# Layer-0 attention stored class by class, two out-projection seams in a new order, and one weight place fewer

## The chip, the cores and the metric

The kernel runs on one core of a Trainium2 chip. The core has a matrix engine (TensorE, in the trace PE, with its weight loads as PEld), a vector engine (VectorE, DVE), an activation engine (ScalarE, ACT), a general engine (GpSimd, POOL), and SyncE (SP), which here only issues DMAs. The engines run their own instruction streams and meet at semaphores. On-chip memory is SBUF (128 partitions), and matmuls write PSUM. The metric is the device time of one execution in microseconds (us); lower is better.

## The reference

Two pre-norm residual layers over 1024 tokens of width 1024, then a final norm. Layer 0 mixes tokens with 12 heads of dilated window attention and a gated MLP; layer 1 with two kinds of dense attention. Each layer ends in a mixture of 16 experts in which experts choose tokens. The part that the change touches most is the dilated attention:

```python
A_PATTERNS = ((128, 1), (512, 4), (2048, 16))
...
def dilated_band_attention(q, k, v, window, dilation):
    """Centred dilated window: query t attends t + j*dilation, |j| <= window/(2*dilation).
...
def dilated_mixture(q, k, v):
    results = [dilated_band_attention(q, k, v, w, d) for (w, d) in A_PATTERNS]
    outs = jnp.stack([o for (o, _) in results], axis=0)
    lses = jnp.stack([l for (_, l) in results], axis=0)
    wts = jax.nn.softmax(lses, axis=0)
    return jnp.einsum('pbsh,pbshc->bshc', wts.astype(q.dtype), outs)
...
def mixer_even(h, pos, w_in, gmlp_norm, w_s, b_s, w_out):
    ...
    return jnp.concatenate([a_out, g_out], axis=-1) @ w_out
...
    for i in range(DEPTH):
        h = rmsnorm(x, norm_mix[i])
        ...
        x = x + mix
        x = x + ec_moe(rmsnorm(x, norm_ffn[i]), moe_w_router[i], moe_w_gate[i], moe_w_up[i], moe_w_down[i])
    return rmsnorm(x, final_norm)
```

## The kernel before

**Products.** float32 operands are split into a high and a low part (`split`: ACT copies the high part, DVE or POOL subtracts for the low one), and a product is three matmuls: high x high, low x high, high x low (L259 to L261). Weights come from HBM in pieces of 128x1024 through a ring of SBUF places; `Stream.load` issues a piece's DMA on SP as soon as a place is free, and `Stream.conv` makes its two parts (L225 hi on ACT, L232 lo on DVE, or on POOL with `pool=True`).

**Attention of layer 0** (`a_attention`). The patterns with dilation 4 and 16 fall together on the positions of one residue class modulo 4, so a head has two kinds of 128-query blocks: eight natural ones (neighbouring positions) and eight class ones (positions r, r+4, r+8 ...; two blocks for each of 4 residues). One unit is two blocks, so a head has 8 units: s < 4 are class units, s >= 4 natural ones. For each unit PE computes scores (`emit_S`, L1190, tile ass: per block two matmuls of 128x256, against the two halves kT[:, 0] and kT[:, 1] of the split keys), DVE masks and takes the maximum (L1192, tile sm), ACT exponentiates (L1199, pe), PE transposes (L1206, apP), ACT copies to SBUF (L1208, pT), and PE multiplies by the values (`emit_PV`, L1220, apO), which come in natural order (vn) and in class order (vc). The hand-written loop over t runs these steps skewed by a unit or two, so that engines work on different units.

The queries and keys of a pair of heads are loaded into qs and ks in natural order (`a_keys`). `prep` splits them for each head (ksp, qsp), transposes them on PE (tile apt) and copies the result to kT and qT (L1139 on DVE, L1141 on ACT); two DMAs (`a_swap`) exchange the halves of kT. In kT and qT positions are in natural order, so a natural unit reads them contiguously, and a class unit reads every fourth element, which is a step of 16 bytes:

```python
out.append((qT.rearrange("p (l r) -> p r l", r=4)[:, r, j * 128:(j + 1) * 128],
            [kT[:, f, 64:64 + S].rearrange("p (l r) -> p r l", r=4)[:, r] for f in range(2)],
```

When a pair is done, its class results go through DRAM into natural order (`bounce`: o2d, then tile o2, shown as o), and `merge` (L1244 to L1272) weighs the natural and the class result by their softmax sums into the tile attn. The merge of an earlier pair is spread over steps of the next; that of the last pair stands behind the loop in two slices of token chunks.

**Seam to the out-projection of layer 0.** The out-projection (`out_moe`, tile pp) multiplies the transposed attn (aTh, aTl, from `mix.part`: PE transposes, L148 and L149 split) by the output weights. Their first pieces are converted in the last steps of attention; four more low parts are made by POOL (`pool=layer == 0`). The first token chunk's products begin with the columns that earlier pairs have filled, and need the last pair's merge from the fifth 128 columns on.

**Seam to the out-projection of layer 1.** Dense attention (`odd_attention`) has 128 blocks: scores css (L1873), maximum (L1879), exponential pe (L1885), transposes cpt, the split PT (L148 and L149), and PV into po (L1915, L1916) in groups of four blocks; L1921 and L1923 add the two halves (ol, o), and the reciprocal row sums rinv go through DRAM (rd, rb). The transposed results lie in DRAM: oda for 14 heads (7 chunks of 128 rows), odb for the last two. `OddMix.load` brings a token chunk back as aT (L1983 for oda, L1984 for odb), into the out-projection's own pool, and `OddMix.part` splits it. The odd output weights' parts lie in three slots of the tile cT.

**Ring places.** The ring has `n_ring = 7` places; further places are added for each layer (8 in layer 0, 15 in layer 1, from the pool ringa), and buffers that have become free join.

## Time and profile before

| | |
|---|---|
| median of 3 runs | 2000.86 us (2000.85 to 2000.86) |
| profiled execution | 1999.71 us, of it 1997.9 us span |
| mean granted TensorE clock | 0.968 of full |
| PE busy | 1864.8 us (93%) |
| DVE, ACT, POOL busy | 1473.5, 1244.9, 352.4 us |

The profile is one execution. The span runs from the first to the last instruction. Busy time is the time in which an engine executed something; the idle time in front of an instruction is put down to the event that ended it. An instruction's line can be that of a helper, so that L232 is the low part of any weight piece and L148 any split.

### The profile page before, as it was taken

The numbers are of one execution on the slowest core, as the hardware profiler recorded it, in microseconds if no ns is written. First come the engines' busy times: TensorE is split into PE (matmuls) and PEld (weight loads), VectorE is DVE, ScalarE is ACT, GpSimd is POOL, SyncE is SP. The second block draws the span as 40 slices with busy tenths as digits, with TensorE's granted clock in tenths as the row PEclk, the third lists the DMA queues.
The fourth block names the chain that finished last, engine by engine and source line by source line (L and its number), as shares of the span: only waits on it lengthen the run. The fifth ranks groups of instructions, "written<-read, shape, count | busy, mean of one in ns | idle before, by whom it ended". The sixth has DMA issues, their size and how long they took to land. (4 is left out here: it accounts for less than half of the span.)

```text
span 1997.9 us, 29943 instructions
## 1 busy us (share of the span) xinstructions
PE 1864.8 (93%) x10346; PEld 1568.7 (79%) x10346; DVE 1473.5 (74%) x3160; ACT 1244.9 (62%) x2022; POOL 352.4 (18%) x337
## 2 busy tenths in 40 slices
PE   8999999998995999998999799999997995999995
PEld 6888899997883788886888688888886873888884
DVE  6431246777557999997776688889996558999997
ACT  5322257776232888886634688889885334888884
POOL 0010010002002321211002233322212003212111
PEclk9999999999996999999899899999998997999997
DMA  7232354543473999995426554332213875999986
GB/s 236 69 106 75 116 153 130 140 108 109 158 261 126 377 389 384 385 395 156 134 70 202 114 75 90 60 50 42 53 22 93 288 256 201 391 387 385 387 332 229
DMA packets 214599, 386.32 MB, mean 193 GB/s; under 512 B 71984, under 2 KB 122928, under 8 KB 214448
## 3 DMA queue, kind: packets, MB, share of 16 engines
q1 hardware_dynamic: 190224, 303.95, 46.0%
q0 software_dynamic: 21488, 74.18, 12.2%
q10 hardware_dynamic: 2736, 6.29, 0.9%
q8 instruction: 81, 1.33, 0.3%
q14 instruction: 70, 0.57, 0.2%
HBM read 310.17 MB, written 66.85 MB: 189 GB/s over the span
## 5 line engine op out<-in xcount | busy, mean ns | idle before, releaser
L232 DVE TENSOR_TENSOR lo<-raw,hi 128x1024 fp32r<-128x1024 f32 x260 | 310.1, 1227 | 24.2 <-ACT hi L225 23.0
L225 ACT ACTIVATE hi<-raw 128x1024 fp32r<-128x1024 f32 x269 | 275.2, 1055 | 14.5 <-PE py L643 10.2
L259 PE MATMUL pp<-hi,hT 128*128 128x512 f32 (+2 forms) x576 | 213.4, 371 | 2.3 <-ACT hi L235 2.3
L260 PE MATMUL pp<-lo,hT 128*128 128x512 f32 (+2 forms) x576 | 211.8, 368 | 0.1
L261 PE MATMUL pp<-hi,hT 128*128 128x512 f32 (+2 forms) x576 | 211.4, 367 | 0.0
L1879 DVE TENSOR_REDUCE nm<-css 128x1 f32<-128x1024 f32 x128 | 156.0, 1218 | 41.5 <-PE css L1873 40.8
L149 DVE TENSOR_TENSOR PT<-cpt,PT 128x512 fp32r<-128x512 f32 x256 | 163.1, 678 | 6.1 <-ACT PT L148 3.8
L148 ACT ACTIVATE PT<-cpt 128x512 fp32r<-128x512 f32 x256 | 139.5, 597 | 42.1 <-PE cpt L1897 40.3
L1873 PE MATMUL css<-kT,qT 128*128 128x512 f32 x512 | 151.7, 398 | 10.7 <-ACT pe L1885 9.5
L1885 ACT ACTIVATE pe<-css,nm 128x1024 f32<-128x1024 f32 x128 | 143.6, 1122 | 11.0 <-DVE rinv L1905 7.1
L1897 PE MATMUL cpt<-csident,pe 128*128 128x128 f32 x1024 | 135.5, 275 | 1.0 <-DVE PT L149 0.9
L1897 PEld LDWEIGHTS cpt<-csident,pe 128*128 128x128 f32 x1024 | 117.1, 141 | 16.3 <-DVE PT L149 3.7
L1915 PE MATMUL po<-PT,vv 128*128 128x512 f32 x256 | 113.4, 443 | 13.2 <-DVE o L1923 13.2
L259 PEld LDWEIGHTS pp<-hi,hT 128*128 128x128 f32 x576 | 109.7, 190 | 19.8 <-ACT hi L235 2.7
L260 PEld LDWEIGHTS pp<-lo,hT 128*128 128x128 f32 x576 | 109.6, 190 | 17.8 <-DVE lo L236 0.8
L261 PEld LDWEIGHTS pp<-hi,hT 128*128 128x128 f32 x576 | 109.4, 190 | 17.5 <-DVE hT L149 0.2
L1873 PEld LDWEIGHTS css<-kT,qT 128*128 128x128 f32 x512 | 96.0, 189 | 34.6 <-ACT pe L1885 10.8
L1192 DVE CUSTOM_DVE_ANT_0 sm<-ass,csnat 128x256 f32<-128x256 f32 x176 | 67.3, 420 | 52.0 <-PE ass L1190 45.9
L578 POOL DMA_INDIRECT xs<-hd,idx x32 | 70.2, 2195 | 197.5 <-DVE gt L576 197.5
L1916 PE MATMUL po<-PT,vv 128*128 128x512 f32 x256 | 102.3, 400 | 0.0
L1190 PE MATMUL ass<-kT,qT 128*128 128x256 f32 x384 | 96.4, 381 | 1.0 <-DMA kT<-kT 1.0
L259 PE MATMUL pp<-hi,aTh 128*128 128x512 f32 x208 | 87.3, 420 | 0.4 <-DVE o L1226 0.4
(435 smaller groups left out, 4656.0 us busy)
## 6 DMA issues: line engine op xcount, KB each, us to landing
raw<-in_moe_w_up_dram SPq DMA_DIRECT2D x112, 512.0 KB
raw<-in_moe_w_down_dram SPq DMA_DIRECT2D x110, 512.0 KB
raw<-in_moe_w_gate_dram SPq DMA_DIRECT2D x106, 512.0 KB
attn<-in_moe_w_gate_dram SPq DMA_DIRECT2D x22, 512.0 KB
attn<-in_moe_w_down_dram SPq DMA_DIRECT2D x18, 512.0 KB
raw<-in_even_w_in_dram SPq DMA_DIRECT2D x16, 512.0 KB
hd<-h POOLq DMA_DIRECT2D x16, 512.0 KB, 6.0
attn<-in_moe_w_up_dram SPq DMA_DIRECT2D x16, 512.0 KB
```

Of the source, the lines that this page charges most:

```text
L148: self.nc.scalar.activation(hi, src, AF.Copy)
L149: (eng or self.nc.vector).tensor_tensor(lo, src, hi.bitcast(F32), op=ALU.subtract)
L225: nc.scalar.activation(hv, tv, AF.Copy)
L232: (nc.gpsimd if pool else nc.vector).tensor_tensor(lv, tv, hv.bitcast(F32), op=ALU.subtract)
L259: nc.tensor.matmul(out, ah, bh, start=first, stop=False)
L260: nc.tensor.matmul(out, ah, bl, start=False, stop=False)
L261: nc.tensor.matmul(out, al, bh, start=False, stop=last)
L1873: nc.tensor.matmul(ss[:, n], a[:, sl], m[:, n * 512:(n + 1) * 512], start=(j == 0), stop=(j == len(passes) - 1))
L1879: nc.vector.tensor_reduce(nm, B[b]["ss"], axis=AX.X, op=ALU.max, negate=True)
L1885: nc.scalar.activation(pe, B[b]["ss"], AF.Exp, bias=B[b]["nm"], accum_out=l)
L1897: nc.tensor.transpose(pt[:, kk], B[b]["pe"][:, kc * 128:(kc + 1) * 128], k.ident)
L1915: nc.tensor.matmul(po[g], vv[:, kc], PT[g][:, 0, kc], start=(kc == 0), stop=False)
```

## The change

First, layer 0's attention is stored class by class. Queries and keys are loaded in class order (four DMAs for ks, then four for qs, instead of one each), so kT and qT hold the four residue classes one behind the other, kT with 16 zero elements on both sides of each class. A class unit reads contiguous columns. A natural unit reads its keys as runs of 32 elements, its mask's columns and its values' rows are permuted to that order (vn comes by 12 DMAs instead of 3), and its queries come from a second copy qN, which is written back into natural order, every fourth element (for head 0 on DVE, for the other 11 heads on ACT, two copies each).

Second, at the seam to layer 0's out-projection POOL makes one low part and DVE the others, and the last merge is cut after 2 chunks instead of 4. Third, at the seam to layer 1's out-projection aT gets a pool of its own (mixa), and the load from oda is issued inside attention, at `late[-4]`. Fourth, the ring has 6 places; layer 0 gets 9 instead of 8 further ones, layer 1 15 as before.

```diff
+    wk = 128 * (w // 128) + 4 * (w % 32) + w % 128 // 32
...
-        add(name, np.where(ok, 0.0, NEG))
+        add(name, np.where(ok, 0.0, NEG)[:, wk])
...
-            stream.conv(base + (4 if layer else 8), pool=layer == 0, load=False)
+            if layer == 0:
+                stream.conv(base + 5, pool=True, load=False)
+            stream.conv(base + (4 if layer else 7), load=False)
...
+PAD = 16
...
-    nc.sync.dma_start(qs, src[:, c:c + 128].rearrange("(c p) d -> p c d", p=128))
-    nc.sync.dma_start(ks, src[:, w + c:w + c + 128].rearrange("(c p) d -> p c d", p=128))
+    for t, c0 in ((ks, w + c), (qs, c)):
+        v = src[:, c0:c0 + 128].rearrange("(f p r) d -> p r f d", f=2, r=4)
+        for r in range(4):
+            nc.sync.dma_start(t[:, 2 * r:2 * r + 2], v[:, r])
...
-    nc.gpsimd.memset(vn[0:64, 0], 0.0)
-    nc.gpsimd.memset(vn[64:128, 8], 0.0)
+    nc.gpsimd.memset(vn[:, 0], 0.0)
+    nc.gpsimd.memset(vn[:, 8], 0.0)
...
-    nc.sync.dma_start(vn[64:128, 0], vv[0:64])
-    nc.sync.dma_start(vn[:, 1:8], vv[64:960].rearrange("(c p) d -> p c d", p=128))
-    nc.sync.dma_start(vn[0:64, 8], vv[960:1024])
+    for r in range(4):
+        p = 32 * r
+        nc.sync.dma_start(vn[p + 16:p + 32, 0], vv[0:64].rearrange("(l r) d -> r l d", r=4)[r])
+        nc.sync.dma_start(vn[p:p + 32, 1:8], vv[64:960].rearrange("(c l r) d -> r l c d", l=32, r=4)[r])
+        nc.sync.dma_start(vn[p:p + 16, 8], vv[960:1024].rearrange("(l r) d -> r l d", r=4)[r])
...
-        nc.sync.dma_start(*(kT[p:p + 64, f, 64:64 + S].bitcast(F32) for p, f in ((64 - a, 1), (a, 0))))
+        nc.sync.dma_start(*(kT[p:p + 64, f, :, PAD:PAD + 256].bitcast(F32) for p, f in ((64 - a, 1), (a, 0))))
+def a_pads(nc, kT):
+    nc.vector.memset(kT[:, :, :, 0:PAD].bitcast(F32), 0.0)
+    nc.vector.memset(kT[:, :, :, PAD + 256:].bitcast(F32), 0.0)
+def two(v):
+    return v.rearrange("p (r l) -> p r l", r=2)
...
-    kT, qT = take("kT", 2, 128 + S, dtype=F32R), take("qT", S, dtype=F32R)
+    kT, qT, qN = take("kT", 2, 4, 2 * PAD + 256, dtype=F32R), take("qT", S, dtype=F32R), take("qN", S, dtype=F32R)
...
-    pair, head = dict(qs=qs, ks=ks, cls=cls), dict(kT=kT, qT=qT)
+    pair, head = dict(qs=qs, ks=ks, cls=cls), dict(kT=kT, qT=qT, qN=qN)
...
-    def trans(n, dst):
+    def trans(n, dst, nat=None):
...
-            pv, sl = pt.rearrange("p a d -> p (a d)"), slice(half * 512, (half + 1) * 512)
+            pv, rs = two(pt.rearrange("p a d -> p (a d)")), slice(2 * half, 2 * half + 2)
...
-                nc.vector.tensor_copy(dst[:, sl], pv)
+                nc.vector.tensor_copy(dst[:, rs], pv)
...
-                nc.scalar.activation(dst[:, sl], pv, AF.Copy)
+                nc.scalar.activation(dst[:, rs], pv, AF.Copy)
+            if nat is not None:
+                nc.vector.tensor_copy(nat[:, rs], pv)
...
-        trans(0, kT[:, 0, 64:64 + S])
-        nc.vector.memset(kT[:, :, 0:64].bitcast(F32), 0.0)
-        nc.vector.memset(kT[:, :, 64 + S:].bitcast(F32), 0.0)
+        trans(0, kT[:, 0, :, PAD:PAD + 256])
+        a_pads(nc, kT)
...
-        trans(1, qT)
+        trans(1, qT.rearrange("p (r l) -> p r l", r=4), qN.rearrange("p (l r) -> p r l", r=4))
...
-                d["kT"] = pk.tile([128, 2, 64 + S + 64], F32R, name="kT")
-                nc.vector.memset(d["kT"][:, :, 0:64].bitcast(F32), 0.0)
-                nc.vector.memset(d["kT"][:, :, 64 + S:].bitcast(F32), 0.0)
+                d["kT"] = pk.tile([128, 2, 4, 2 * PAD + 256], F32R, name="kT")
+                a_pads(nc, d["kT"])
...
+                d["qN"] = pk.tile([128, S], F32R, name="qN")
...
-            def tr(dst, src, eng):
+            def tr(dst, src, eng, nat=None):
...
-                pv = pt.rearrange("p a d -> p (a d)")
+                pv = two(pt.rearrange("p a d -> p (a d)"))
...
+                if nat is not None:
+                    late.append(lambda: nc.scalar.activation(nat, pv, AF.Copy))
...
-                tr(d["kT"][:, 0, 64 + half * 512:64 + (half + 1) * 512], lambda c: d["ksp"][:, 4 * half + c], half)
+                tr(d["kT"][:, 0, 2 * half:2 * half + 2, PAD:PAD + 256], lambda c: d["ksp"][:, 4 * half + c], half)
...
-                tr(d["qT"][:, half * 512:(half + 1) * 512], lambda c: d["qsp"][:, 4 * half + c], True)
+                rs = slice(2 * half, 2 * half + 2)
+                tr(d["qT"].rearrange("p (r l) -> p r l", r=4)[:, rs], lambda c: d["qsp"][:, 4 * half + c], True,
+                   d["qN"].rearrange("p (l r) -> p r l", r=4)[:, rs])
...
-            qT, kT = d["qT"], d["kT"]
+            qT, qN, kT = d["qT"], d["qN"], d["kT"]
...
-                    out.append((qT[:, c * 128:(c + 1) * 128], [kT[:, f, c * 128:c * 128 + 256] for f in range(2)],
+                    out.append((qN[:, c * 128:(c + 1) * 128],
+                                [kT[:, f, :, 32 * c:32 * c + 64].rearrange("p r (a l) -> p a r l", a=2) for f in range(2)],
...
-                    out.append((qT.rearrange("p (l r) -> p r l", r=4)[:, r, j * 128:(j + 1) * 128],
-                                [kT[:, f, 64:64 + S].rearrange("p (l r) -> p r l", r=4)[:, r] for f in range(2)],
+                    out.append((qT[:, 256 * r + j * 128:256 * r + (j + 1) * 128],
+                                [kT[:, f, r, PAD:PAD + 256] for f in range(2)],
...
+                o = ss[:, j] if len(ks[0].shape) == 2 else ss[:, j].rearrange("p (a r l) -> p a r l", a=2, r=4)
...
-                    nc.tensor.matmul(ss[:, j], q, ks[f], start=(f == 0), stop=(f == 1))
+                    nc.tensor.matmul(o, q, ks[f], start=(f == 0), stop=(f == 1))
...
-        merge(NP - 1, slice(0, 4))
+        merge(NP - 1, slice(0, 2))
...
-        merge(NP - 1, slice(4, 8))
+        merge(NP - 1, slice(2, 8))
...
-        out_moe(k, 0, stream, at, cva, 4, 8, 4, mix[0], lambda c: x_in[c * 128:(c + 1) * 128], xres, hd)
+        out_moe(k, 0, stream, at, cva, 4, 9, 4, mix[0], lambda c: x_in[c * 128:(c + 1) * 128], xres, hd)
...
-    def __init__(self, k, od):
-        self.k, self.od, self.t, self.a = k, od, {}, {}
+    def __init__(self, k, od, pool):
+        self.k, self.od, self.t, self.a, self.pa = k, od, {}, {}, pool
...
+    def load_a(self, c):
+        a = self.a[c] = self.pa.tile([128, NCH, 128], F32, name="aT", bufs=1)
+        self.k.nc.sync.dma_start(a[:, 0:7], self.od[0][:, c * 128:(c + 1) * 128].rearrange("(k p) t -> p k t", p=128))
...
-        a = self.a[c] = self.pool.tile([128, NCH, 128], F32, name="aT", bufs=1)
-        sl = slice(c * 128, (c + 1) * 128)
-        self.k.nc.sync.dma_start(a[:, 0:7], self.od[0][:, sl].rearrange("(k p) t -> p k t", p=128))
-        self.k.nc.sync.dma_start(a[:, 7], self.od[1][:, sl])
+        if c not in self.a:
+            self.load_a(c)
+        self.k.nc.sync.dma_start(self.a[c][:, 7], self.od[1][:, c * 128:(c + 1) * 128])
...
+        mix = OddMix(k, od, ctx.enter_context(tc.tile_pool(name="mixa", bufs=1, side="right", reuse_waits="tile")))
...
-            odd_attention(k, H[0], od, keys, {-12 + 3 * j: [lambda j=j: (stream.conv(at["out"] + j, load=False), stream.load(at["out"] + 8))] for j in range(1, 4)})
-        out_moe(k, 1, stream, at, cva, 3, 15, 5, OddMix(k, od), lambda c: xin[c * 128:(c + 1) * 128], xres, hd, out)
+            late = {-12 + 3 * j: [lambda j=j: (stream.conv(at["out"] + j, load=False), stream.load(at["out"] + 8))] for j in range(1, 4)}
+            late[-4] = [lambda: mix.load_a(0)]
+            odd_attention(k, H[0], od, keys, late)
+        out_moe(k, 1, stream, at, cva, 3, 15, 5, mix, lambda c: xin[c * 128:(c + 1) * 128], xres, hd, out)
...
-        n_ring = 7
+        n_ring = 6
```

How the instructions stand then on the engines, at three places. First ACT while head 2 of layer 0 is prepared: kT, pe, pT, ksp, qsp as above, qN the new copy. Before:

```order
L1141 ACTIVATE kT<-apt 128x512
L1199 ACTIVATE pe<-sm,o_2336 128x256 x2
L1208 ACTIVATE pT<-apP 128x512
L1199 ACTIVATE pe<-sm,o_2336 128x256 x2
L1208 ACTIVATE pT<-apP 128x512
L1199 ACTIVATE pe<-sm,o_2336 128x256 x2
L1208 ACTIVATE pT<-apP 128x512
L148 ACTIVATE ksp<-ks 128x8x64
```

And with the change:

```order
L1165 ACTIVATE kT<-apt 128x2x256
L1229 ACTIVATE pe<-sm,o_2352 128x256 x2
L1238 ACTIVATE pT<-apP 128x512
L1229 ACTIVATE pe<-sm,o_2352 128x256 x2
L1238 ACTIVATE pT<-apP 128x512
L1167 ACTIVATE qN<-apt 128x2x256
L1229 ACTIVATE pe<-sm,o_2352 128x256 x2
L1238 ACTIVATE pT<-apP 128x512
L1167 ACTIVATE qN<-apt 128x2x256
L150 ACTIVATE ksp<-ks 128x8x64
```

The two qN copies stand between pT's in the steps between one head's kT and the next head's ksp; nothing else on ACT moves there.

Second, DVE behind the last unit of layer 0's attention (o_4710 and o_4831 are the last pair's natural result, o_5108 and o_5234 the class result that comes back from DRAM; aTl is the low part of the first half of token chunk 0). Before:

```order
L149 TENSOR_TENSOR aTl<-apP,aTh 128x512
L1226 COPY o_4710<-apO 128x4x65
L1244 TENSOR_TENSOR dd<-o_4710,o_5108 128x8
L1245 TENSOR_TENSOR mm<-dd,o_4710 128x8
...
L1264 TENSOR_TENSOR o_4710<-o_4710,ww 128x8x64
L1268 TENSOR_TENSOR attn<-o_5108,ww 128x4x128
L1272 TENSOR_TENSOR attn<-attn,o_4710 128x4x128
L149 TENSOR_TENSOR aTl<-apP,aTh 128x512
```

And with the change:

```order
L151 TENSOR_TENSOR aTl<-apP,aTh 128x512
L1256 COPY o_4831<-apO 128x4x65
L234 TENSOR_TENSOR lo<-raw,hi 128x1024
L1274 TENSOR_TENSOR dd<-o_4831,o_5234 128x4
L234 TENSOR_TENSOR lo<-raw,hi 128x1024
L1275 TENSOR_TENSOR mm<-dd,o_4831 128x4
...
L1294 TENSOR_TENSOR o_4831<-o_4831,ww 128x4x64
L1298 TENSOR_TENSOR attn<-o_5234,ww 128x2x128
L1302 TENSOR_TENSOR attn<-attn,o_4831 128x2x128
L151 TENSOR_TENSOR aTl<-apP,aTh 128x512
```

Two low parts of weight pieces have come in, one ahead of the merge and one behind its first operation, and the merge's operations have half the width. On POOL, four low parts in a row have become one.

Third, ACT at the end of layer 1's attention (pe and PT belong to the last blocks, cT is the high part of an output weight, aTh the split of the loaded aT). Before:

```order
L1885 ACTIVATE pe,l<-css,nm 128x1024
L148 ACTIVATE PT<-cpt 128x4x128 x2
L225 ACTIVATE cT<-raw 128x1024
L1885 ACTIVATE pe,l<-css,nm 128x1024
L148 ACTIVATE PT<-cpt 128x4x128 x2
L148 ACTIVATE aTh<-aT 128x512
L148 ACTIVATE PT<-cpt 128x4x128 x2
L1921 ACTIVATE ol<-po 64x512 x2
```

And with the change:

```order
L1915 ACTIVATE pe,l<-css,nm 128x1024
L150 ACTIVATE aTh<-aT 128x512
L150 ACTIVATE PT<-cpt 128x4x128 x2
L227 ACTIVATE cT<-raw 128x1024
L1915 ACTIVATE pe,l<-css,nm 128x1024
L150 ACTIVATE PT<-cpt 128x4x128 x4
L1951 ACTIVATE ol<-po 64x512 x2
```

The split of aT now stands ahead of two pairs of PT, one cT and one pe that it stood behind. On SP's queue the load of aT keeps its neighbours, with one more weight load ahead of it. Before:

```order
L204 DMA raw<-in_odd_w_out_dram 128x2x512
L1925 DMA rb<-rd 64x512
L1908 DMA rd<-rinv 128x4x1
L1925 DMA rb<-rd 64x512
L1983 DMA aT<-oda 128x7x128
L1908 DMA rd<-rinv 128x4x1
```

And with the change:

```order
L206 DMA raw<-in_odd_w_out_dram 128x2x512
L1955 DMA rb<-rd 64x512
L1938 DMA rd<-rinv 128x4x1
L206 DMA raw<-in_odd_w_out_dram 128x2x512
L1955 DMA rb<-rd 64x512
L2012 DMA aT<-oda 128x7x128
L1938 DMA rd<-rinv 128x4x1
```

Between the last rd before aT and aT itself one `raw` load has come in.

## Rows read from the trace of the kernel before

**Rows 1.** The page's totals: busy us of each engine, share, instructions.

```profile
PE 1864.8 (93%) x10346; PEld 1568.7 (79%) x10346; DVE 1473.5 (74%) x3160; ACT 1244.9 (62%) x2022; POOL 352.4 (18%) x337
```

**Rows 2.** Stretches: us, busy PE, PEld, DVE, ACT, POOL, then PEclk, DMA share, GB/s.

```profile
270.00:486.00 216.00, 214.51 (x1726) 212.64 (x1724) 149.33 (x563) 157.17 (x334) 12.90 (x18) 1.00 0.45 117
...
1676.00:1967.00 291.00, 288.71 (x1428) 233.87 (x1428) 275.01 (x305) 243.28 (x276) 61.50 (x30) 1.00 0.98 367
...
341.20:376.30 35.10, 35.10 (x288) 35.06 (x288) 24.60 (x95) 25.29 (x55) 2.26 (x3) 1.00 0.48 120
...
499.00:502.00 3.00, 3.00 (x12) 2.67 (x11) 1.40 (x7) 1.25 (x3) 0.00 (x0) 0.54 0.00 0
```

**Rows 3.** Timeline of PE in layer 0's attention: start, us, instruction.

```profile
356.48 0.72 PE L1190 MATMUL ass<-kT,qT 128*128 128x256 f32 x4
357.04 1.00 PE L1220 MATMUL apO<-vn,pT 128*128 128x65 f32 x8
...
358.24 1.29 PE L1190 MATMUL ass<-kT,qT 128*128 128x256 f32 x4
359.35 1.02 PE L1220 MATMUL apO<-vn,pT 128*128 128x65 f32 x8
```

**Rows 4.** Timelines of POOL, DVE, PE at layer 0's out-projection; in brackets idle time before.

```profile
485.95 7.04 POOL L232 TENSOR_TENSOR lo<-raw,hi 128x1024 fp32r<-128x1024 f32 x3 [23.06 <-ACT hi L225]
...
488.92 1.79 DVE L1244 TENSOR_TENSOR dd<-o,o 128x8 f32<-128x8 f32 x1 [2.37 <-DMA o<-o2d]
...
494.99 2.83 DVE L1268 TENSOR_TENSOR attn<-o,ww 128x512 f32<-128x512 f32 x1
...
500.86 0.16 DVE L1244 TENSOR_TENSOR dd<-o,o 128x8 f32<-128x8 f32 x1
...
504.33 0.69 DVE L1272 TENSOR_TENSOR attn<-attn,o 128x512 f32<-128x512 f32 x1
...
498.68 0.90 PE L1363 MATMUL apP<-csident,attn 128*128 128x128 f32 x3 [7.61 <-DVE attn L1272]
```

**Rows 5.** Timelines of DVE, SP, ACT, PE at layer 1's out-projection, the same columns.

```profile
1504.70 1.23 DVE L232 TENSOR_TENSOR cT<-raw,cT 128x1024 fp32r<-128x1024 f32 x1
...
1511.13 0.36 SPq L1983 DMA_DIRECT2D aT<-oda  x1
...
1538.12 0.37 SPq L1983 DMA_DIRECT2D aT<-oda  x1
...
1523.88 0.63 ACT L148 ACTIVATE aTh<-aT 128x512 fp32r<-128x512 f32 x1 [8.21 <-DMA aT<-oda]
...
1543.82 1.15 ACT L148 ACTIVATE aTh<-aT 128x512 fp32r<-128x512 f32 x2 [4.28 <-DMA aT<-oda]
...
1527.08 0.80 PE L1915 MATMUL po<-PT,vv 128*128 128x512 f32 x1 [8.93 <-DVE o L1923]
...
1533.39 0.39 PE L259 MATMUL pp<-cT,aTh 128*128 128x512 f32 x1
```

**Rows 6.** Groups by tile (gpm, pp): ns min, median, max; first and last start; form.

```profile
L259 PE MATMUL gpm<-vh,wT x4: 388/390/397, 114.2 to 133.1; 128*128 128x512 f32 x4
...
L259 PE MATMUL pp<-hi,hT x53: 392/397/400, 100.2 to 139.4; 128*128 128x512 f32 x53
```

**Rows 7.** The same view of the tile kT, 270 to 486 us.

```profile
L1141 ACT ACTIVATE kT<-apt x11: 582/585/592, 278.7 to 450.6; 128x512 fp32r<-128x512 f32 x11
```

**Rows 8.** The page's costliest groups: busy us, mean ns, idle before and its releaser.

```profile
L232 DVE TENSOR_TENSOR lo<-raw,hi 128x1024 fp32r<-128x1024 f32 x260 | 310.1, 1227 | 24.2 <-ACT hi L225 23.0
...
L1190 PE MATMUL ass<-kT,qT 128*128 128x256 f32 x384 | 96.4, 381 | 1.0 <-DMA kT<-kT 1.0
```

**Rows 9.** The tile h: ACT's copy that reads at 8-byte steps.

```profile
L399 ACT ACTIVATE h<-xt,rstd x2: 1194/1195/1196, 614.8 to 1646.6; 128x1024 f32<-128x1024 f32 x2
```

**Rows 10.** Timeline of SP in layer 0's attention.

```profile
352.05 3.26 SPq L1013 DMA_DIRECT2D vc<-vd  x4
```

**Rows 11.** Waits of SP, 1495 to 1530: us in total, times, longest.

```profile
SPq L1983 <- PE css L1873: 6.5, 1, 6.5
```

## The prediction

> **What bounds the kernel now.** I read the page's totals first: TensorE (PE) is busy 93% of the 1997.9 us span, DVE 74%, ACT 62% [rows 1]. An average hides the stages, so next the busy times by stretch. In the first layer's attention, 270 to 486 us, PE is busy 214.5 of 216 us while the DMA share is 0.45 [rows 2]: what PE does paces this stage, and only shorter PE work or a new wait can change it. The last expert stage is full too (288.7 of 291 us), at a DMA share of 0.98 [rows 2]. The list of PE's instructions inside attention then shows the one odd thing. A natural unit takes 0.56 us from its score matmuls (L1190) to its PV matmuls (356.48 to 357.04), a class unit 1.11 us (358.24 to 359.35) for the same four matmuls of 128x256 [rows 3]. The two differ only in that class units read queries and keys at every fourth element, 16 bytes apart. Last, the two seams: PE stands 7.61 us before 498.68 [rows 4] and 8.93 us before 1527.08 [rows 5], and starts at a low clock after each.
>
> **Attention: what is removed.** 12 heads have 4 class units each, so 48 class groups. Each gets contiguous reads and, if it then costs what a natural group costs, saves 1.11 - 0.56 = 0.55 us [rows 3]: 48 x 0.55 = 26.4 us.
> The natural units now read keys as runs of 32 elements with gaps. Do such runs cost? No row has runs of 32; the nearest is the gMLP product, whose moving operand is in runs of 64 and takes 0.390 us against 0.397 for a plain one of the same width [rows 6]. So I take nothing. The other bound is the stride's full price, 48 natural groups x 0.55 = 26.4 us lost, which would cancel the gain.
>
> **Attention: what is added.** Eleven heads get two more ACT copies each (qN, 128x512, from PSUM), which write every fourth element. If such a copy costs what the kT copy costs, 0.585 us [rows 7], a pair of heads takes ACT from 25.29 [rows 2] to 25.29 + 4 x 0.58 = 27.6 us, while the pair's 35.1 us of PE [rows 2] falls by 8 x 0.55 to 30.7. ACT is then 90% busy, DVE with its 24.6 us [rows 2] 80%. Both stay below PE, but not evenly, and three losses follow.
> (i) Bursts on DVE: a merge puts two operations of 128x1024 (some 1.2 us each by the nearest row of that size, L232's [rows 8]) and eight small ones into four of the pair's sixteen steps, each now 1.8 to 2.1 us. I put 0.6 us lost per merge, 5 merges inside the stage, 3 us (0 to 6.7).
> (ii) Bursts on ACT: the splits and the kT and qN copies of one head lie in five successive steps; at 0.585 they just fit. I allow 1.5 us in all, and 2 us for the last steps, where the output weights' conversions (hi on ACT, lo on DVE) are mixed in.
> (iii) The first swap of kT's halves already causes PE's only wait for a DMA here, 1.0 us [rows 8], and now has less work in front of it: 0.8 us more.
> Attention gives 26.4 - 3 - 3.5 - 0.8 = **19 us**, from 12 to 25.
> What does the write at 16-byte steps cost? No row of before has an ACT write like it. From below: the contiguous 0.585. From above: PE's factor of two at the same step, 1.17 us. The nearest ACT row is a copy that reads at 8-byte steps, 1.194 us for 1024 elements [rows 9], against 2 x 0.585 for two of 512: no penalty seen. It is an ACT row and so nearer than PE's; I take 0.6.
> The Trainium skill says in "Advanced Engine Details and Errata", section "SBUF Cachelines", that SBUF is accessed in lines of 16 bytes and that full speed needs at least two hits in a line. For reads by PE the trace agrees (1.11 against 0.56 us); for a write by ACT no run shows it, and by the rule each qN copy would pay. This speaks for the class half of the change and against its qN half; the result is rival (a).
>
> **Attention: loads.** Per pair SP now issues 24 DMAs (8 for keys and queries, 4 + 12 for values) instead of 9. An issue takes from 0.36 us (aT's [rows 5]) to 0.8 (four vc ones 3.26 [rows 10]), so the burst takes 9 to 19.6 us, say 14. Keys go first, in four parts, so the last is issued about when the whole is now. Behind the burst on SP's queue stands the next head's swap, seven steps or some 14 us after the burst's start: just clear, and I put it at nothing. At 0.8 per issue it is 5 us late against about 4 us of slack, a price of 1 to 2 us for each of 5 pairs.
> The wider memsets lie on POOL, 18% busy [rows 1]; permuted masks cost nothing.
>
> **Seam to the first out-projection.** POOL makes three low parts from 485.95 on (7.04 us for three), and DVE's merge crawls beside them: its 128x512 operation takes 2.83 us while POOL makes a fourth, where an operation of that shape in the second merge, with POOL silent, takes 0.69 [rows 4]. The first merge and its follow-up last from 488.92 to PE's start at 498.68, 9.8 us; the second, undisturbed, with 0.7 us of another operation in it, from 500.86 to 505.02 [rows 4], 4.2 us. Now POOL keeps one low part, over at about 488.3; DVE makes the next two at 1.23 us each [rows 8], and the merge ahead of PE covers 2 chunks instead of 4, which takes three operations from 0.69 to about 0.4 us.
> In sequence: low part 5 from 488.3 to 489.5, the first merge operation, low part 6 to 490.9, the rest of the merge 2.3 to 2.7 us, so 493.2 to 493.6 against 498.68: 5.1 to 5.5 us.
> With a pause of some 2.5 us instead of 7.6 the clock should not fall. Before, PE ran at 0.54 of full speed from 499 to 502 [rows 2], so 3 x 0.46 = 1.4 us come back. Against this, the low part of piece 7 now stands on DVE's path: 0.4 us. Sum: **6.5 us**, from 3 (POOL's part still overlaps the merge) to 7.5. The remaining six-chunk merge lies under the first token chunk's matmuls, as the four-chunk one does now.
>
> **Seam to the second out-projection.** SP issues the load of aT (448 KB) at 1511.13 [rows 5], after 6.5 us of waiting for PE's scores [rows 11]: aT's place is free only then. ACT's split of it starts at 1523.88, after 8.21 us of standing [rows 5]. Behind that split on ACT stand PT of the last block and ol, so DVE's add, then PE: its last sixteen PV matmuls start at 1527.08 at half clock (0.80 us for the first against 0.39 for one of that width at 1533.39) and take 6.31 us, until out-projection begins at 1533.39 [rows 5].
> With a place of its own the load needs no such wait. SP reaches it behind one weight load and one rb, just after DVE frees that weight's slot (1504.70 + 1.23 = 1505.93 [rows 5]): 1506.9. The transfer's length is bounded by two in the trace: 12.7 us (1511.13 to 1523.88) and 5.7 (1538.12 to 1543.82) [rows 5]. So it lands between 1512.6 and 1519.6; I take 8 us, 1515.
> But the split has moved ahead as well. ACT now reaches its place at 1523.88 - 8.21 = 1515.7; the two pairs of PT (four of 0.58, as [rows 7]), cT's high part and one exp (1.1 each, somewhat under [rows 9]) that it overtakes are 4.5 us, so ACT reaches it at 1511.2 and stalls to 1515. Then the split 0.6, a pair of PT 1.2, cT 1.1, exp 1.1, two pairs 2.3, ol 0.6 and DVE's add 0.7: 7.6 us, 1522.6. PE's last PV takes from there 3.5 (clock kept) to 6.3 us; the middle, 1527.5, against 1533.39 is **6 us**, from 0 (a landing at 1519.6, low clock) to 9.
>
> **One weight place fewer.** The rings hold 27 places in the first layer as before and 26 instead of 27 in the second. In its expert stage PE hardly stands [rows 2]: the store of loaded pieces isn't empty. I put 0; at most one piece comes late, 0.5 MB at 367 GB/s [rows 2], 1.4 us.
>
> **Sum.** 19 + 6.5 + 6 = 31.5 us. The profiled execution took 1999.71 us (span 1997.9 and 1.8 around it), which gives 1968; the median of the runs shown is 1.15 us above it: **1969 us**.
>
> **Rivals.**
> (a) ACT becomes the bound: qN copies at 1.17 us. In the five steps of a head that hold them ACT then needs 10.9 us against PE's 9.8 (five steps of 1.76 or, with transposes, 2.1 us): 1.1 us for each of 11 heads, 12 us off the gain, **1981 us**. For it: PE's factor of two. Against it: the 8-byte row.
> (b) Runs of 32 cost like stride, the units only change roles, and just the seams gain: **1988 us**. Against it: the 64-runs.
> (c) SP's burst makes the swap late, 2 us for each of 5 pairs: **1979 us**. For it: vc's 0.8 us per issue.
> (d) aT lands late, since the transfer shares the queues with weights and attention's own loads, and seam 2 gives nothing: **1975 us**. For it: 12.7 us for the present load.
> (e) Slower: the strided write costs four times, 2.3 us a copy. ACT then needs 25.3 + 4 x 2.3 = 34.5 us a pair, and its copies lie in bursts that hold up the exps. It decides from where those stalls exceed the rest of the gain, 38 us or 3.5 a head: **2005 us** or more above that. Against it: no ACT row shows a factor above 1.1.
>
> **How the numbers follow.** Chances: the forecast 0.60, (a) 0.15, (c) 0.07, (d) 0.09, (b) 0.05, (e) 0.03, no change to speak of by some mixture 0.01. The forecast's terms (12 to 25, 3 to 7.5, 0 to 9, not all at one end) give 1960 to 1976 for itself. The range reaches to (a), (c) and (d) and leaves (b) and (e) out: 1959 to 1984. This measurement can tell about 0.2%, 4 us, from no change; all cases but (e) and the mixture lie further below 2000.86. So faster 0.96, same 0.01, slower 0.03.
>
> **What would show it.** Right: class and natural units both at 0.56 us from scores to PV, a pair near 31 us, PE over 95% busy in attention, qN copies at 0.58 to 0.62 us (at 1.17 (a) is right, with exps waiting behind them). At the first seam a merge without a 2 us operation, a pause of PE of about 2.5 us, and full clock behind it. At the second aT issued right behind the low part that frees the weight's slot, landed before the last exp, PE's pause under 6 us. Wrong: PE waiting for pe or pT through attention, swaps behind vn's issues, a split of aT after 1519.

## The result and the profile after

The changed kernel takes 1990.37 us (median of 4 runs, 1987.64 to 1991.01) against 2000.86 us for the kernel before: a ratio of 0.9942, with a 95% interval of 0.9925 to 0.9959. That is 10 us faster, where 32 were forecast. The profiled execution took 1990.35 us, of it 1988.6 us span. On a second chip, unaltered, it had 0.9956 (0.9935 to 0.9977). The kernel before itself had medians from 1992.7 to 2003.0 us on the chips used below, so runs are compared by their ratio to it on the same chip, and places in the program by the profiles.

The totals of the page and two stretches, with the columns of [rows 1] and [rows 2]; the first stretch is one pair of heads in attention, as 341.2 to 376.3 was before, the second lies in attention's last steps:

```profile
PE 1846.5 (93%) x10346; PEld 1542.3 (78%) x10346; DVE 1475.7 (74%) x3165; ACT 1259.7 (63%) x2044; POOL 343.5 (17%) x334
```

```profile
305.87:339.36 33.49, 32.71 (x291) 31.19 (x290) 25.05 (x97) 27.94 (x60) 3.10 (x4) 1.00 0.60 152
```

```profile
450.00:462.00 12.00, 9.87 (x53) 9.16 (x53) 7.84 (x25) 8.27 (x16) 1.92 (x1) 0.65 0.00 1
```

A pair went from 35.1 to 33.5 us, not to 31. PE is no longer always busy in it (32.7 of 33.5), and in the last steps its granted clock falls to 0.65 of full, where it was 1.00 over all of attention before [rows 2].

PE's timeline in attention, answering [rows 3]: a class unit (qT), then a natural one (qN).

```profile
341.53 0.72 PE L1220 MATMUL ass<-kT,qT 128*128 128x256 f32 x4
342.09 1.00 PE L1250 MATMUL apO<-vc,pT 128*128 128x65 f32 x8
...
345.39 0.72 PE L1220 MATMUL ass<-kT,qN 128*128 128x256 f32 x4
345.94 1.00 PE L1250 MATMUL apO<-vc,pT 128*128 128x65 f32 x8
```

Both take 0.55 to 0.56 us from scores to PV: the class units have got the natural price and the natural ones kept it. The loss is on ACT. The copies by tile (as [rows 7]), and the waits from 297 to 470 us (total, times, longest):

```profile
L1167 ACT ACTIVATE qN<-apt x22: 1068/1097/1116, 282.6 to 456.2; 128x512 fp32r<-128x512 f32 x22
```

```profile
ACT qN L1167 <- DVE qT L1163: 13.2, 11, 1.3
PEld apP L1236 <- ACT pe L1229: 12.3, 35, 2.3
```

A qN copy takes 1.10 us, not 0.6. All 22 start behind DVE's copy of qT from the same transposes, and eleven times ACT stands 1.2 us in front of one until that copy has ended, with the next exp queued behind it. In the last steps this ends in a visible pause, and PE starts again at half clock (timelines of ACT and PE):

```profile
451.72 1.08 ACT L1167 ACTIVATE qN<-apt 128x512 fp32r<-128x512 f32 x1 [1.08 <-DVE qT L1163]
452.58 1.06 ACT L227 ACTIVATE hi<-raw 128x1024 fp32r<-128x1024 f32 x1
453.54 0.90 ACT L1229 ACTIVATE pe<-sm,o 128x256 f32<-128x256 f32 x2
```

```profile
454.09 1.12 PE L1236 MATMUL apP<-csident,pe 128*128 128x128 f32 x4 [2.13 <-ACT pe L1229]
```

The first seam, answering [rows 4] (timelines of DVE and PE): one DVE low part still runs beside POOL's and takes 2.57 us, the next 1.21; the merge's operations are undisturbed, and PE's pause is 2.26 us instead of 7.61, with the clock at 1.00 in the 4 us behind it.

```profile
479.65 2.57 DVE L234 TENSOR_TENSOR lo<-raw,hi 128x1024 fp32r<-128x1024 f32 x1 [0.30 <-ACT hi L227]
...
485.20 0.42 DVE L1298 TENSOR_TENSOR attn<-o,ww 128x256 f32<-128x256 f32 x1
```

```profile
486.13 0.55 PE L1393 MATMUL apP<-csident,attn 128*128 128x128 f32 x3 [2.26 <-DVE attn L1302]
```

The second seam, answering [rows 5], on SP, ACT and PE; and two rows of SP from the kernel before that the prediction had not used:

```profile
1492.09 0.41 SPq L2012 DMA_DIRECT2D aT<-oda  x1
1508.95 0.36 SPq L1938 DMA_DIRECT2D rd<-rinv  x1
...
1524.42 0.34 SPq L2017 DMA_DIRECT2D aT<-odb  x1
```

```profile
1505.04 0.63 ACT L150 ACTIVATE aTh<-aT 128x512 fp32r<-128x512 f32 x1 [8.72 <-DMA aT<-oda]
...
1507.48 1.12 ACT L1915 ACTIVATE pe<-css,nm 128x1024 f32<-128x1024 f32 x1
...
1526.86 0.31 ACT L150 ACTIVATE aTh<-aT 128x128 fp32r<-128x128 f32 x1 [6.38 <-DMA aT<-odb]
```

```profile
1506.94 1.97 PE L1927 MATMUL cpt<-csident,pe 128*128 128x128 f32 x8 [9.02 <-DVE PT L151]
...
1518.33 0.39 PE L261 MATMUL pp<-cT,aTh 128*128 128x512 f32 x1
...
1528.16 0.50 PE L261 MATMUL pp<-hi,aTh 128*128 128x512 f32 x1 [3.10 <-ACT hi L227]
```

```profile
1514.97 0.36 SPq L1908 DMA_DIRECT2D rd<-rinv  x1
...
1530.98 0.34 SPq L1984 DMA_DIRECT2D aT<-odb  x1
```

The load is issued early, as forecast, but lands 12.9 us later. ACT waits for it at the split, and a pair of PT and the last exp (1507.48) stand behind. PE's pause has only moved: it is 9.02 us ahead of the next transposes, which wait for PT, where 8.93 us stood before the last PV. From that exp hang the last reciprocals (rd), their way through DRAM (rb), the last outputs (odb) and their load as aT's last 128 rows. Counted from the last score matmul (1510.7 before, 1495.7 now), rd goes out after 13.3 us instead of 4.3, and odb is loaded after 28.7 instead of 20.3. Out-projection begins 22.7 us after the last scores, as before. Then ACT waits for odb (1526.86) with weight conversions queued behind that split, so PE stands 3.10 us and another 0.76, and its clock is 0.72 from 1527 to 1533.

### The profile page after: what moved, and what is told of

Its sections match the earlier page's. It is cut to its first block, busy times and chain, and to the rows that moved or that the text cites. A ratio compares the mean times of both kernels' runs of the same rounds, so it can differ in the third digit from the quotient of the medians.

```text
span 1988.6 us, 30142 instructions
## 1 busy us (share of the span) xinstructions
PE 1846.5 (93%) x10346; PEld 1542.3 (78%) x10346; DVE 1475.7 (74%) x3165; ACT 1259.7 (63%) x2044; POOL 343.5 (17%) x334
## 4 chain that ended last, share of the span: by engine, by line
PE 41%; DVE 5%; DMA 3%; ACT 1%; issue 1%; POOL 0%; SPq 0%; ACTq 0%; POOLq 0%; DVEq 0%
PE css L1903 6%; PE cpt L1927 5%; PE py L647 4%; PE pp L261 3%; PE pp L262 3%; PE pp L263 3%; PE po L1945 3%; PE po L1946 2%; PE pg L261 1%; PE pg L262 1%; PE pg L263 1%; PE pu L261 1%; PE pu L262 1%; PE pu L263 1%; DMA widek<-ktc 1%
## 5 line engine op out<-in xcount | busy, mean ns | idle before, releaser
L151 DVE TENSOR_TENSOR PT<-cpt,PT 128x512 fp32r<-128x512 f32 x256 | 163.1, 677 | 15.1 <-ACT PT L150 12.9
L1903 PE MATMUL css<-kT,qT 128*128 128x512 f32 x512 | 151.5, 397 | 10.6 <-ACT pe L1915 9.4
L1915 ACT ACTIVATE pe<-css,nm 128x1024 f32<-128x1024 f32 x128 | 143.7, 1123 | 12.9 <-DVE rinv L1935 9.0
L1927 PE MATMUL cpt<-csident,pe 128*128 128x128 f32 x1024 | 136.9, 277 | 10.7 <-DVE PT L151 10.5
L262 PEld LDWEIGHTS pp<-lo,hT 128*128 128x128 f32 x576 | 109.5, 190 | 17.8 <-DVE lo L238 0.8
L150 ACT ACTIVATE xh<-tp 128x512 fp32r<-128x512 f32 x64 | 38.2, 600 | 78.1 <-PE tp L592 78.1
```

The costliest lines, as they stand in the source:

```text
L150: self.nc.scalar.activation(hi, src, AF.Copy)
L151: (eng or self.nc.vector).tensor_tensor(lo, src, hi.bitcast(F32), op=ALU.subtract)
L262: nc.tensor.matmul(out, ah, bl, start=False, stop=False)
L1903: nc.tensor.matmul(ss[:, n], a[:, sl], m[:, n * 512:(n + 1) * 512], start=(j == 0), stop=(j == len(passes) - 1))
L1915: nc.scalar.activation(pe, B[b]["ss"], AF.Exp, bias=B[b]["nm"], accum_out=l)
L1927: nc.tensor.transpose(pt[:, kk], B[b]["pe"][:, kc * 128:(kc + 1) * 128], k.ident)
```

## The experiments

Each run's time is given as its ratio to the kernel before on the same chip (95% interval). For where it went there are three stretches of PE's timeline, from the profiles. **A** is attention, from the first score matmul to the first matmul of the out-projection; **B** the first seam, from there to the transposes behind the merge; **C** the second seam, from the last score matmul to one fixed matmul some 48 us into the out-projection.

| run | A us | B us | C us | ratio |
|---|---|---|---|---|
| before | 215.8 | 12.1 | 70.5 | 1 |
| changed | 209.2 | 6.7 | 76.1 | 0.9942 |
| changed, second chip | 210.4 | 7.3 | 76.1 | 0.9956 |
| 1 attention alone | 208.0 | 12.1 | 66.6 | 0.9953 |
| 2 first seam alone | 216.9 | 6.8 | 68.7 | 0.9969 |
| 3 second seam and ring alone | 217.2 | 12.1 | 74.7 | 1.0033 |
| 4 aT's split late | 207.7 | 6.7 | 71.3 | 0.9934 |
| 5 qN contiguous | 200.7 | 6.8 | 75.7 | 0.9928 |
| 6 no qN | 193.9 | 7.0 | 76.7 | 0.9865 |
| 7 qN on POOL | 198.8 | 7.1 | 75.7 | 0.9913 |
| 8 POOL, split late | 199.1 | 7.1 | 70.9 | 0.9882 |
| 10 as 8, third o | 200.5 | 7.0 | 71.0 | 0.9891 |
| 11 as 4, weight load later | 209.6 | 6.8 | 72.9 | 0.9935 |
| 12 qN a step later | 198.3 | 6.7 | 75.4 | 0.9904 |
| 13 as 12, split late | 199.9 | 7.1 | 70.4 | 0.9873 |
| 14 as 12, old second seam | 200.2 | 7.0 | 66.0 | 0.9856 |

(The changed kernel on the second chip is run 9.) The changed kernel's A, B and C sum to 6.4 us less than before's. Most of the remaining 3 us lies between B and the first score matmul of layer 1 (the first layer's experts and the second layer's projections), a stretch that was 3.3 us shorter here and 0.6 to 3.7 us in the other runs; its cause was not followed. Each row is one execution: with attention unchanged, A is 1.1 and 1.4 us longer in runs 2 and 3 than before, and C lies between 66.0 and 70.5 us in the four runs that have the second seam of before (before, 1, 2, 14).

**Run 1, attention alone.** The changed kernel with the other parts taken back:

```diff
-            late[-4] = [lambda: mix.load_a(0)]
...
-        merge(NP - 1, slice(0, 2))
+        merge(NP - 1, slice(0, 4))
...
-        n_ring = 6
+        n_ring = 7
```

> The kernel before with the class-by-class attention alone; both seams and the ring are those of before. Theory 1 (the three parts add up, and the second seam is a loss): attention is worth the 7 us by which PE reached the first out-projection early, so about 1993.5 us. Rival (the seam's reordering is what eats attention's gain, since weights are converted inside attention's last steps in both): the same 12 or more us as up to 447 us in the profile, 1989 us. If ring and seams were worth nothing it would equal the changed kernel, 1990.4 us.

0.9953 (0.9936 to 0.9971), 7.9 us by the medians: theory 1. A falls by 7.8 us.

**Run 2, the first seam alone,** on the kernel before:

```diff
-            stream.conv(base + (4 if layer else 8), pool=layer == 0, load=False)
+            if layer == 0:
+                stream.conv(base + 5, pool=True, load=False)
+            stream.conv(base + (4 if layer else 7), load=False)
...
-        merge(NP - 1, slice(0, 4))
+        merge(NP - 1, slice(0, 2))
```

> The kernel before with only the first seam's new order (one low part on POOL instead of four, the merge cut at 2 chunks). Theory 1: PE's pause falls from 7.6 to about 2.3 us and the clock stays, 5.5 to 6 us, 1995 us. Rival (the pause is short only because attention's end has moved): under 2 us gained, 1999 us or more.

0.9969 (0.9959 to 0.9979), 6.1 us by the medians, of which 5.3 lie in B. This run also tells something of the second seam, which it leaves as it was (timelines of ACT, DVE and PE):

```profile
1509.39 0.63 ACT L148 ACTIVATE aTh<-aT 128x512 fp32r<-128x512 f32 x1 [0.79 <-DMA aT<-oda]
```

```profile
1517.65 0.68 DVE L1925 TENSOR_TENSOR o<-po,ol 64x512 f32<-64x512 f32 x1 [5.70 <-DMA odb<-o]
```

```profile
1518.38 0.79 PE L1917 MATMUL po<-PT,vv 128*128 128x512 f32 x1 [7.31 <-DVE o L1925]
```

Here aT was there almost in time (issued at 1504.06, 5.3 us), and PE stood 7.31 us before its last PV all the same: DVE's o waited until the store of an older o (odb) had freed its place, which hangs on rb. So PE's pause of 8.93 us in [rows 5] was not the price of aT's load alone.

**Run 3, the second seam and the ring alone,** on the kernel before: the class OddMix of the changed kernel, and

```diff
+            late[-4] = [lambda: mix.load_a(0)]
...
-        n_ring = 7
+        n_ring = 6
```

> The kernel before with only aT's own pool, its early load and 6 ring places. Theory 1: a loss of about 5.5 us, 2006 us, with the last exp of attention behind the split of aT and the load of odb issued some 8.5 us later, measured from the last scores, than before. Rival (the loss of the changed kernel behind its second seam comes from elsewhere): no loss, 1998 to 2001 us.

1.0033 (1.0023 to 1.0044), 5.6 us slower: theory 1. The last exp stands behind the split as in the changed kernel, and odb is loaded 26.6 us after the last scores. The parts of runs 1 to 3 add up to 8.5 us gained; the whole has 10.5.

**Run 4, aT's split late:** the same load, but the split queued on ACT behind the output copy ol of the last group but one.

```diff
-            nc.scalar.activation(ol, po[g][64:128], AF.Copy)
+            ins = nc.scalar.activation(ol, po[g][64:128], AF.Copy)
+            if g == 30:
+                k.tail = ins
...
-            mix.part(0, 0)
+            if layer:
+                with tc.issue_after(k.tail.ins):
+                    mix.part(0, 0)
+            else:
+                mix.part(0, 0)
```

> The changed kernel, with aT's first split queued on ACT behind the output copy ol of the last group but one, so that no exp and no PT stands behind it. Theory 1 (the place of the split costs, not the load): the last exp, the reciprocals and the load of odb come some 9 us earlier, PE reaches the out-projection 4 to 8 us earlier; 5.6 to 13 us less than the changed kernel, 1978 to 1985 us. Rival (the load of aT, 12.9 us long, is what PE waits for, wherever the split stands): within 2 us of 1990.4.

0.9934 (0.9917 to 0.9951). C falls from 76.1 to 71.3 us: in the profile the place of the split costs 5 us. PE does not reach the out-projection earlier, as theory 1 had it (23.7 us after the last scores, 22.7 in the changed kernel); what is gained lies behind that, where odb is loaded 21.4 us after the last scores instead of 28.7. By the ratios the gain over the changed kernel is 2 to 4 us, less than theory 1 expected, and not clear of the intervals on its own.

**Run 5, qN written contiguously** (natural blocks then use queries in another order, so part of the output is another):

```diff
-                   d["qN"].rearrange("p (l r) -> p r l", r=4)[:, rs])
+                   d["qN"].rearrange("p (r l) -> p r l", r=4)[:, rs])
```

> The changed kernel, with ACT's qN copies written contiguously (the natural blocks' queries then stand in class order, so the output is another); count, place and waits of the copies are as before. Theory S (the write at 16-byte steps is what attention lost): a copy falls from 1.10 to 0.58 us, 22 x 0.5 = 11 us off ACT, of which PE gets 4 to 9 us: 1981 to 1986 us. Rival W (the copies' wait for DVE's qT copy holds ACT up, whatever they cost): under 3 us gained, 1988 us or more.

A copy takes 0.597 us, and A falls by 8.4 us, to 200.7, although the waits for DVE's qT copy are still there (14.4 us in 16 times). So theory S holds for attention in the profile. The ratio of all executions, 0.9928 (0.9903 to 0.9953), is 3 to 6 us below the changed kernel's, which its interval does not tell from nothing; in the profiled execution dense attention was 2.6 us longer than in the changed kernel's.

**Run 6, no qN copies on ACT** (natural blocks read class-ordered queries, the output is another):

```diff
-                if nat is not None:
-                    late.append(lambda: nc.scalar.activation(nat, pv, AF.Copy))
```

> The changed kernel without ACT's qN copies for heads 1 to 11 (the natural blocks read class-ordered queries, so the output is another). Both theories: the whole of what the copies cost attention comes back, about 12 us, 1978 us, and a pair of heads near 31 us. Under S most of that is already in the run with contiguous copies; under W most of it is only here. A third possibility, that PE's own work (runs of 32 keys) eats the gain: within 3 us of 1990.4.

A is 193.9 us, 21.9 less than before. The ratio is 0.9865 (0.9829 to 0.9901).

**Run 7, qN made by POOL** from the finished qT, and **run 8**, the same with run 4's late split:

```diff
-                    late.append(lambda: nc.scalar.activation(nat, pv, AF.Copy))
+                    late.append(lambda: nc.gpsimd.tensor_copy(nat, dst))
```

> The changed kernel, with qN made by POOL from the finished qT in SBUF instead of by ACT from PSUM (22 POOL copies, seven steps ahead of their use). S and W alike: ACT is free of both the write and the wait, about 10 us gained, 1980 us. Against it: POOL's strided copies beside DVE's operations could slow DVE as at the first seam of before; then under 4 us, 1987 us or more, with DVE operations of two SBUF sources over 1 us long.

> qN on POOL and the late split of aT together: if the two mechanisms are separate their gains add up; with 10 us from the one and 6 to 13 from the other, 1968 to 1975 us. If either is not the cause, no better than the other alone.

```profile
L1167 POOL CAST qN<-qT x22: 1120/1153/2102, 283.4 to 450.5; 128x512 fp32r<-128x512 f32 x22
...
L1298 DVE TENSOR_TENSOR attn<-o,ww x5: 2302/2547/2598, 315.9 to 449.4; 128x1024 f32<-128x1024 f32 x5
```

POOL's copies take 1.15 us, need nothing of ACT, and A falls to 198.8. What was expected against it came too: the first large product of each merge on DVE takes 2.5 us beside POOL (second row; 1.21 us in the changed kernel), but it did not eat the gain. The ratios are 0.9913 (0.9880 to 0.9945) and 0.9882 (0.9848 to 0.9916): the two repairs add up in the profiles, at 4.8 us of C for the second, though both times are 4 to 5 us longer than expected.

**Run 9, the changed kernel again:**

> The changed kernel unaltered, to have its time on the chip of the three next to it: 0.994 of the kernel before, as measured at first.

0.9956; its A, B and C repeat those of the first profile within 1.2 us.

**Run 10, a third place for o:** run 8 with

```diff
-            ol = pol.tile([64, 512], F32, name="ol")
+            ol = pol.tile([64, 512], F32, name="ol", bufs=1)
-            o = pol.tile([64, 512], F32, name="o")
+            o = pol.tile([64, 512], F32, name="o", bufs=3)
```

> qN on POOL, the late split of aT, and three places instead of two for the tile o of the last attention's outputs (ol gets one instead of two). With the late split PE waited 9.7 us before its last PV for DVE's o, and that for the store of an older o (odb). If that chain of rb, o and odb is what the second seam is bound by, the wait goes and 4 to 8 us more are gained than by POOL and the late split alone: 0.980 to 0.985 of before. If the seam is bound by the last reciprocals' way through DRAM (rd, rb, odb, aT), PE starts earlier but waits later for odb, and the time is that of the run without the third place, 0.988.

0.9891 (0.9866 to 0.9915), and C is unchanged at 71.0. PE reached out-projection 10.6 us sooner than in run 8 (12.7 instead of 23.3 us after the last scores), and then ACT waited as much longer for odb (waits from 1480 to 1525 us):

```profile
ACT aTh L150 <- DMA aT<-odb: 10.5, 1, 10.5
```

So here the seam ends with the last blocks' way through DRAM, whenever PE starts.

**Run 11, the weight load ahead of rb issued later:** run 4 with

```diff
-            late = {-12 + 3 * j: [lambda j=j: (stream.conv(at["out"] + j, load=False), stream.load(at["out"] + 8))] for j in range(1, 4)}
+            late = {-12 + 3 * j: [lambda j=j: (stream.conv(at["out"] + j, load=False), j < 2 and stream.load(at["out"] + 8))] for j in range(1, 4)}
```

> The changed kernel with the late split, and the weight load that stood on SP ahead of rb and aT's early load issued only with the out-projection. If that load is what makes aT take 12.9 us and the rb beside it 12 us to land, both land within 6 us, and the second seam gains 4 to 9 us against the late split alone: 0.985 to 0.989 of before. If not, the landings stay near 12 us and the time is that of the late split, 0.9934, or worse by a late weight.

0.9935 (0.9910 to 0.9960). PE's last PV began 7 us earlier than in run 4, counted as above, and odb was loaded 17.1 us after the last scores instead of 21.4. But ACT then waited 3.2 us for odb and 7.6 us for a late weight piece, which took that back: C is 72.9. No gain.

**Run 12, each qN copy one step later,** when DVE is done with the same transposes:

```diff
-        late = []
+        late, later = [], []
...
-                    late.append(lambda: nc.scalar.activation(nat, pv, AF.Copy))
+                    later.append(lambda: nc.scalar.activation(nat, pv, AF.Copy))
...
-            late.clear()
+            late[:] = later
+            later.clear()
```

> The changed kernel with each qN copy on ACT one step later, when DVE's copy of the same transposes is done: the copies still cost 1.10 us each, only their waits (13.2 us in the profile of the changed kernel) go. Theory W (waiting for DVE is a part of what the copies cost): 3 to 7 us less than the changed kernel, 0.991 to 0.9925 of before. If the strided write is all: within 2 us of the changed kernel.

0.9904 (0.9879 to 0.9929): theory W. The copies still take 1.11 us each, none waits for DVE, A falls by 10.9 us to 198.3, and the last steps keep their clock (stretch, then waits, as above):

```profile
450.00:462.00 12.00, 11.46 (x103) 11.12 (x102) 8.31 (x33) 10.52 (x22) 0.00 (x0) 1.00 0.09 25
```

```profile
PEld apP L1236 <- ACT pe L1229: 4.3, 14, 0.7
```

**Run 13, run 12 with the late split, and run 14, run 12 with the second seam and the ring of before:**

> The changed kernel with both repairs that leave the amount of work alone: each qN copy on ACT one step later, and aT's split behind the last-but-one ol. If the two causes are separate, the 10 us of the one and the 5 us by which PE's steps from the last scores into the out-projection were shorter with the late split add up: 0.986 to 0.989 of before. If the late split pays only where something else holds up ACT, 0.990, as with the later copies alone.

> The same later qN copies, with the second seam and the ring of the kernel before (no early load of aT, no pool of its own, 7 ring places). If the early load is worth nothing even with its split out of the way, because the last blocks' way through DRAM binds the seam, this takes the same time as the run beside it with the late split, within 3 us. If the early load is worth the 6 us that were predicted for it, this one is 5 us or more slower.

0.9873 (0.9849 to 0.9898) and 0.9856 (0.9830 to 0.9883), medians of 1976.49 and 1971.91 us on one chip. The early load with its split out of the way shows no gain: by the medians run 14, without it, is 4.6 us shorter, which the intervals do not tell apart, and in the profiles C is 70.4 with it and 66.0 without. PE's pause before its last PV, in run 13 and in run 14:

```profile
1503.59 0.79 PE L1950 MATMUL po<-PT,vv 128*128 128x512 f32 x1 [10.18 <-DVE o L1960]
```

```profile
1495.82 0.51 PE L1946 MATMUL po<-PT,vv 128*128 128x512 f32 x1 [1.81 <-DVE o L1954]
```

Run 14 has the lowest ratio of all, with class-by-class storage, the first seam's order, and each qN copy a step later; runs 6, 8 and 13 lie within its interval.

## Why the prediction was wrong

**What held.** The strided read was what class units paid, and runs of 32 cost nothing: both kinds of unit stand at 0.56 us. Without qN on ACT attention gains 21.9 us (run 6) of the 26.4. The difference, 4.5, is near the 3.8 of the terms (i) and (iii), but no run shows that it is theirs: PE's one wait for a swap, term (iii), was 0.5 us in the changed kernel where it had been 1.0. No other swap was waited for, so rival (c) did not come. The first seam was forecast at 6.5 and gave 6.1 us (run 2), with a pause of 2.26 us for the forecast 2.5 and no fall of the clock. One ring place fewer cost the experts nothing that shows: behind C the span goes on for 416.8 us, 416.7 before.

**Attention's term was 19 and measured 6.6 us; the step that failed is the price and the cover of the qN copies, "I take 0.6" and "1.5 us in all".** Two things are behind it. The copy takes 1.10 us, near the upper bound that I had and put into rival (a). And the copy waits: ACT reads the transposes only after DVE has read them, so a DVE burst (a merge) passes straight on to ACT and to the exps behind. That wait has no term in the sum. Either repair alone gives more than half of the loss back (run 5: 8.4 us; run 12: 10.9; no copies at all, run 6: 15.3), so the two losses do not add up. My reading is that either one lets ACT's burst fit into PE's steps; no run shows that by itself. With neither, PE pauses 2.13 us in the last steps and its clock is low behind it (the 2.26 us of the first seam left it at 1.00), and from some 32 us before attention's end to that end PE loses 4.5 us against its place before; it is 1.0 in run 5 and nothing in run 12. Rival (a) forecast 12 us off attention's gain, and 12.4 is what went. That the two agree is in part luck: run 12 keeps the price of 1.11 us and is 10.9 us better, so most of the loss needs the wait, which rival (a) did not have.

The Trainium skill's rule in "Advanced Engine Details and Errata", section "SBUF Cachelines", was the better guide to this write than the 8-byte row, and the trace agrees with it: 1.10 us at 16-byte steps against 0.597 for the same copy written contiguously.

**The second seam's term was a gain of 6 and measured a loss of 5.6 us; the step that failed is the taking of aT's landing as what PE waits for.** The profile shows 8.21 us of ACT waiting for it in [rows 5], and that was true of that execution: it took 12.7 us to land. But a second chain ends at about the same time: the last reciprocals, rd, rb, o, odb. Run 2, with the same order, shows PE nearly as long at a stand with aT landed in 5.3 us. In runs 1 and 14, again with the same order, aT landed in 4.7 us at most and in 5.2 us, the older o was stored in time, and PE reached out-projection 12.7 and 14.6 us after the last scores instead of 22.7: the pause that the forecast set out to remove varied with the execution. Run 10 shows that starting PE 10 us sooner gives nothing while odb comes no earlier. What C goes with is the moment at which odb is loaded, counted from the last scores: 17.8 to 20.3 us with the order of before (C 66.0 to 70.5), 21.4 to 23.4 with the early load and the late split (C 70.4 to 71.3), 26.6 to 28.7 with the changed order (C 74.7 to 76.7); only run 11, with its late weight, stands outside.

Two terms failed with it. The landing was taken as 8 us, between 5.7 and 12.7, and took 12.9, which by the forecast's own sum takes most or all of the gain of 6 (rival (d)); out-projection began no earlier than before. And I listed what stands behind the moved split on ACT (two pairs of PT, cT, an exp) and added up their durations, but did not ask who waits for that exp besides PT. In the sum ACT's stall was harmless because PE had a pause anyway; the chain through DRAM had none to give, and began 9 us later.

**The ring.** The place fewer costs the experts nothing, but it put one more weight load between the last rd but one and its rb on SP's queue, as the order showed. Run 14 has neither that load nor the early aT, and its C is the shortest, 66.0 us. Which of the two makes run 13's C 4.5 us longer was not told apart. Run 11 points at the weight load: without it, and with aT loaded still earlier, odb was loaded 17.1 us after the last scores, as with the order of before.

**The range** treated the rivals as alternatives. Rival (a)'s price came true with a wait beside it, and (d) with a loss on top; each alone lay inside the range, both together do not.

## What to carry to other kernels

When an instruction is moved ahead on an engine, follow the consumers of everything that it now delays to the end of the stage, not only the engine that idles: a chain through DRAM with 20 us of latency can lie hidden behind a pause and become the bound when its head is late. A second reader of a tile can inherit the first reader's lateness, so a cheap extra copy is best issued a step later, or on an engine that nobody waits for, with an eye on what it slows there. Independent risks to independent terms add up, and the range has to hold their joint case.

## What the runs showed of the hardware

An ACT write of 128x512 at 16-byte steps takes 1.10 us against 0.597 contiguous (the changed kernel and run 5), while a PE read at that step took twice as long (1.11 us against 0.56 for a unit) and reading in runs of 32 nothing extra (0.55 to 0.56). DVE pays too: its two qN copies take 1.08 us, its qT copies 0.69 (the changed kernel). POOL writes the same pattern from SBUF in 1.15 us, hardly slower than ACT, and A is as short with it (198.8) as with ACT's copies a step later (198.3), although a DVE product of 128x1024 beside it takes 2.5 us instead of 1.21 (run 7).

The load of aT, 448 KB, took from 4.7 to 13.9 us from issue to split where ACT came to it in time (runs 1 and 10), and the row broadcasts rb beside it up to 13.5 from issue to use (run 10). In the changed kernel the share of the DMA engines was 0.15 and 0.41 in the two 3 us stretches behind the issue at 1492.09, and then 0.70 and 0.88 until the landing, at 112 and 191 GB/s; so they were far from full at first only. Run 11, with one weight load out of the way, did not settle what the loads wait for; it stays open.
